# Feed-forward up stage: the first block of tokens goes through three column tiles before the second block, and three plain pairs instead of two

## The chip, the cores and the metric

One core of one Trainium2 chip. The metric is the device time of one execution in microseconds (us); the median of three runs is given, and one execution is profiled. Clock means the clock granted to TensorE: 1.00 is 2.4 GHz, the lower level is 1.2 GHz.

## The reference

Two layers of a transformer with 1024 latent tokens and, in the first layer only, 256 context tokens that are updated as well. Each layer has a mixing part and then a feed-forward part, which is where the change lies:

```python
h = modulate(rmsnorm(x, norm_ffn_g[layer]), sh2, sc2)
x = x + g2 * conv_ffn(h, ffn_w_up[layer], ffn_conv_w[layer], ffn_conv_b[layer], ffn_w_down[layer])
...
def conv_ffn(h, w_up, cw, cb, w_down):
    u = dwconv3(h @ w_up, cw, cb)
    a, b = jnp.split(u, 2, axis=-1)
    return (jax.nn.silu(a) * b) @ w_down
```

The model width is 1024, the feed-forward width 2816, all in fp32. dwconv3 is a convolution of three taps over the tokens, channel by channel.

## The kernel before

Channels lie on the 128 partitions, tokens along the free dimension: columns 0 to 255 are the context, 256 to 767 the first block of latent tokens (L0), 768 to 1279 the second (L1). Every fp32 product is made of three fp32r matmuls (mm3, lines 145 to 148): each operand is split into a high part (ScalarE, L1012 for weights, L308 for activations) and a low part (VectorE, L1013 and L309), and high x high, high x low and low x high are summed in PSUM.

The feed-forward width is cut in 22 pairs of column tiles of 128: tile j = 0 is of a, tile j = 1 of b. The document writes (i, j) for tile j of pair i. For each pair the kernel computes the product of both tiles with all tokens, runs the convolution (conv, L1026 on ScalarE, L1027 and L1029 on VectorE), the silu and the gate (L1034, L1035), and writes the result to DRAM (L1037, through the queue of SP).

norm_up (L965) comes first. It spills X to DRAM (L972) and then, block by block, makes the mean square (L262 to L267, the sum over partitions is a matmul into a tile of the pool s), the root (L270 to L275, into n_w), the scaled X (L291, in place) and its two parts hh and hl (L308, L309). The blocks are: context (layer 0 only), first block, second block. All but the last block have high priority.

up_plain (L1039) then computes NP0 = 2 pairs by plain products: pair 0 first for the context and for the first block, with both tiles, then for the second block, since the second block's hh and hl are ready last; pair 1 follows with (1,0) and then (1,1). The other 20 pairs are computed in ffn_up (L1083) by seven half-size products in place of eight (L1098 to L1100); they need the sums T1 to T4 of the blocks, which sums_b (L988) makes on VectorE and ScalarE between norm_up and up_plain in program order. T2, T3 and T4 lie in a pool pT, T1 is written over H after the plain pairs.

Weights come by up_load (L1005) into two buffers wst, and up_unit (L1016) splits a tile into whi and wlo, of which there are two each. So the split of (1,0) needs the buffer of (0,0), after that tile's last product.

PSUM has 8 banks. During up_plain they are given as uc = 1 (the context products of both tiles of a pair share it), u = 2 (tiles of two banks, one column tile each), s = 3; then s and u are closed and sx = 2, sy = 3, s = 2 are opened for ffn_up (line 1447 and below). The v tiles that the convolution writes are one per j, in a pool pV which lies where norm_up's scratch lay; a v tile is free again when the gate has read it and, for j = 0, when it has been written to DRAM.

The order of the instructions on each engine is fixed at build time by the framework's planner: it goes by its own estimate of when each instruction could start, and among those that could, by program order, with the blocks under high priority first. On the chip each engine then works through that order and waits on semaphores. In layer 0 the pairs in ffn_up also carry steps of the next layer's modulation (ada_chain, run_background; 17 steps, one a pair).

Of the kernel before, what the change touches and what calls it, by code (L numbers as in the profile page):

```python
# [8 lines left out]
F32 = mybir.dt.float32  # L9
# [5 lines left out]
P = 128  # L15
# [13 lines left out]
TB_END = [(256, 512), (768, 256), (1024, 256)]  # L29
HN = NLAT // 2  # L30
HK = KD // 2
NP0 = 2
L0, L1 = slice(NCTX, NCTX + HN), slice(NCTX + HN, T)


# [30 lines left out]
def kernel_body(ctx, tc, A, n_layers=2):  # L66
# [13 lines left out]
    def open_pool(name, side, bufs=1):  # L80
        return tc.alloc_tile_pool(name=name, bufs=bufs, side=side, reuse_waits="tile")

    def open_psum(**kinds):
        for key, bufs in kinds.items():
            PS[key] = tc.alloc_tile_pool(name="ps" + key, bufs=bufs, space=PSUM, reuse_waits="tile",
                                         side="left" if key == "s" else "right")
# [58 lines left out]
    def mm3(ps, whi, wlo, hhi, hlo, first, last):  # L145
        PE.matmul(ps, whi, hhi, start=first, stop=False)  # L146
        PE.matmul(ps, whi, hlo, start=False, stop=False)  # L147
        PE.matmul(ps, wlo, hhi, start=False, stop=last)  # L148
# [867 lines left out]
    def up_unit(i, j, c0=0):  # L1016
        hi = pW.tile([P, D], F32R, tag="whi", name="whi")
        lo = pW.tile([P, D], F32R, tag="wlo", name="wlo")
        split_w(hi[:, c0:], lo[:, c0:], raw[i, j][:, c0:])
        return hi, lo  # L1020

    def conv(l, i, j, v, u, s0, n):
        f = i + j * FT
        w = prm[l][:, PB_FCW + 3 * f:PB_FCW + 3 * f + 3]
        bi = prm[l][:, PB_FCB + f:PB_FCB + f + 1]
        S.activation(out=v[:, s0:s0 + n], in_=u, func=AF.Identity, scale=w[:, 1:2], bias=bi)  # L1026
        V.scalar_tensor_tensor(out=v[:, s0 + 1:s0 + n], in0=u[:, 0:n - 1], scalar=w[:, 0:1],  # L1027
                               in1=v[:, s0 + 1:s0 + n], op0=ALU.mult, op1=ALU.add)
        V.scalar_tensor_tensor(out=v[:, s0:s0 + n - 1], in0=u[:, 1:n], scalar=w[:, 2:3],  # L1029
                               in1=v[:, s0:s0 + n - 1], op0=ALU.mult, op1=ALU.add)  # L1030

    def gate(l, i, v, t_lo):
        a, b = v[0][:, t_lo:], v[1][:, t_lo:]
        last_silu[0] = S.activation(out=a, in_=a, func=AF.Silu)  # L1034
        V.tensor_tensor(out=a, in0=a, in1=b, op=ALU.mult)  # L1035

        (G if i == FT - 1 else SY).dma_start(out=gd[l][i, :, t_lo:], in_=a)  # L1037

    def up_plain(l, pV, tbs, wa, wb):  # L1039

        ctx_too = tbs[0][0] == 0
        w2 = [wa, wb]
        for i in range(NP0):
            pu, psc = [], None

            def product(j, t0, n):
                o = psc[:, j * NCTX:(j + 1) * NCTX] if t0 == 0 else pu[j][:, t0 - NCTX:t0 - NCTX + n]
                whi, wlo = w2[j]
                for k in range(KD):
                    mm3(o, whi[:, k * P:(k + 1) * P], wlo[:, k * P:(k + 1) * P],  # L1050
                        H[k][0][:, t0:t0 + n], H[k][1][:, t0:t0 + n], k == 0, k == KD - 1)

            v = []

            def finish(j):
                v.append(pV.tile([P, T], F32, tag=f"v{j}", name=f"v{j}"))
                with tc.high_priority():
                    if ctx_too:
                        conv(l, i, j, v[j], psc[:, j * NCTX:(j + 1) * NCTX], 0, NCTX)
                    conv(l, i, j, v[j], pu[j], NCTX, NLAT)  # L1060

            if ctx_too:
                psc = PS["uc"].tile([P, 512], F32, tag="uc", name="uc")
            for j in range(2):
                pu.append(PS["u"].tile([P, 2, 512], F32, tag="u", name="u").rearrange("p b c -> p (b c)"))
                if i == 0 and j == 1:

                    for tb in tbs:
                        product(0, *tb)
                        product(1, *tb)  # L1070
                    finish(0)
                    finish(1)
                elif i > 0:
                    for tb in tbs:
                        product(j, *tb)
                    finish(j)
            if i + 1 < NP0:
                up_load(l, i + 1)
                w2 = [up_unit(i + 1, 0), up_unit(i + 1, 1)]
            with tc.high_priority():  # L1080
                gate(l, i, v, tbs[0][0])

    def ffn_up(l, pU, Tt, tbs):  # L1083
        ctx_too = tbs[0][0] == 0
# [265 lines left out]
    for l in range(n_layers):  # L1350
# [58 lines left out]
        for p in range(3):  # L1409
# [15 lines left out]
            if p == 0:  # L1425
# [18 lines left out]
        pA.release()  # L1444

        close_psum("s", "d")
        open_psum(uc=1, u=2, s=3)
        pT = open_pool("pT", "left")
        Tt = {j: [tuple(pT.tile([P, HN], F32R, tag=f"t{j}{k}{c}", name=f"t{j}") for c in "hl") for k in range(HK)]
              for j in (2, 3, 4)}  # L1450
        pN = open_pool("pN2", "right")
        up_load(l, 0)
        wa, wb = up_unit(0, 0), up_unit(0, 1)
        norm_up(l, pN, tbs)
        pN.release()
        sums_b(l, Tt)
        pV = open_pool("pV", "right")
        up_plain(l, pV, tbs, wa, wb)
        up_load(l, NP0)
        for k in range(HK):  # L1460
            parts((H[k][0][:, L1], H[k][1][:, L1]), X[k][:, L0], None)
# [177 lines left out]
```

## Time and profile before

| | us |
|---|---|
| median of three runs | 3089.65 |
| the three runs | 3087.1, 3096.79, 3089.65 |
| the profiled execution | 3087.57 |
| its span, from the first to the last instruction | 3085.6 |
| TensorE busy | 2903.3 (94%) |
| VectorE busy | 2016.6 (65%) |
| ScalarE busy | 1271.5 (41%) |

Times in the rows are us from the start of the span. Layer 0's up stage begins at about 774, layer 1's at about 2346. A row of the timeline has start, duration, engine, line, operation, output and inputs, shape, count, and in brackets how long the engine was idle before and what released it. A matmul's duration is modelled and reaches over the start of the next one, so the pace of TensorE is read from the distance between starts.

### The profile page before, as it was taken

Reading aid. Unit: us, or ns where it says so; the run is one execution under the profiler, and the core shown is the slowest. Engines: PE = TensorE matmul, PEld = TensorE weight load, DVE = VectorE, ACT = ScalarE, POOL = GpSimd, SP = SyncE. Lnnn points to the kernel's source line nnn. Section 1 sums busy time; section 2 is a strip of 40 time slices with the busy share of each in tenths; the row PEclk is TensorE's granted clock in tenths of the full one; section 3 lists DMA queues with packets and bytes.
Section 4 is the critical chain, followed back from the end, with each engine's and each line's share of the span. In section 5 each row is a group of like instructions: output and inputs, shape, how many; then the busy total and the mean of one; then the engine's idle time right before and its main releaser. Section 6 shows DMA issues by size and latency. Waiting matters only on the chain.

```text
span 3085.6 us, 45198 instructions
## 1 busy us (share of the span) xinstructions
PE 2903.3 (94%) x17362; PEld 2343.6 (76%) x17362; DVE 2016.6 (65%) x3281; ACT 1271.5 (41%) x2350; POOL 227.8 (7%) x395
## 2 busy tenths in 40 slices
PE   6899899999899999989999799899998999998997
PEld 4676678888778888878888676677886788886886
DVE  6245664455866666768777536654548777777776
ACT  5155644354534444432112336644444444443212
POOL 0023331010000000000000003320000000000000
PEclk9999999999999999999999899999999999998998
DMA  6535556452122222243212335557532122224321
GB/s 227 159 93 164 170 175 181 126 140 86 50 88 87 88 88 88 74 158 138 93 59 82 101 100 158 166 176 200 160 90 96 69 82 82 82 82 170 117 82 55
DMA packets 258503, 361.02 MB, mean 117 GB/s; under 512 B 114288, under 2 KB 177136, under 8 KB 258288
## 3 DMA queue, kind: packets, MB, share of 16 engines
q1 hardware_dynamic: 258000, 356.95, 36.5%
q8 instruction: 137, 2.24, 0.3%
q0 software_dynamic: 288, 1.18, 0.1%
q14 instruction: 78, 0.64, 0.1%
HBM read 276.92 MB, written 81.13 MB: 116 GB/s over the span
## 4 chain that ended last, share of the span: by engine, by line
PE 74%; DVE 5%; ACT 2%; DMA 2%; issue 1%; POOL 1%; SPq 1%; DVEq 0%; ACTq 0%; POOLq 0%
PE sx L1098 5%; PE sx L1100 5%; PE sx L1099 5%; PE sy L1098 4%; PE sy L1099 4%; PE sy L1100 4%; PE uc L1099 1%; PE uc L1100 1%; PE uc L1098 1%; PE u L146 1%; PE u L147 1%; PE u L148 1%; DMA x<-xf 0%; DVE n_acc L266 0%; DVE wlo L142 0%
## 5 line engine op out<-in xcount | busy, mean ns | idle before, releaser
L141 ACT ACTIVATE whi<-wst 128x1024 fp32r<-128x1024 f32 (+1 forms) x112 | 112.7, 1023 | 465.6 <-DMA wst<-wdn 44.3
L142 DVE TENSOR_TENSOR wlo<-wst,whi 128x1024 fp32r<-128x1024 f32 (+1 forms) x112 | 132.3, 1184 | 96.6 <-ACT whi L141 94.5
L1012 ACT ACTIVATE whi<-wst 128x1024 fp32r<-128x1024 f32 x88 | 84.1, 958 | 114.8 <-PE uc L1099 70.7
L1013 DVE TENSOR_TENSOR wlo<-wst,whi 128x1024 fp32r<-128x1024 f32 x88 | 96.8, 1102 | 49.1 <-ACT whi L1012 49.1
L1012 ACT ACTIVATE s34h<-wst 128x1024 fp32r<-128x1024 f32 x40 | 42.4, 1061 | 166.5 <-PE sy L1099 163.0
L1108 DVE TENSOR_TENSOR ca<-sy,ca 128x512 f32<-128x512 f32 x80 | 55.3, 691 | 75.2 <-PE sy L1100 75.2
L1099 PE MATMUL uc<-hl,whi 128*128 128x256 f32 x320 | 90.6, 283 | 0.0
L1100 PE MATMUL uc<-hh,wlo 128*128 128x256 f32 x320 | 90.5, 283 | 0.0
L1098 PE MATMUL uc<-hh,whi 128*128 128x256 f32 x320 | 90.4, 282 | 0.0
L1037 POOL DMA_DIRECT2D gd<-v x2 | 1.4, 684 | 1168.0 <-DVE v L1035 1168.0
L1013 DVE TENSOR_TENSOR s12l<-s,s12h 128x1024 fp32r<-128x1024 f32 x40 | 49.0, 1225 | 45.5 <-ACT s12h L1012 45.5
L825 POOL TENSOR_SCALAR a_dg<-c_ident,a_sm 128x128 f32<-128x128 f32 x108 | 43.0, 398 | 444.1 <-DVE a_sm L821 311.8
L1104 ACT ACTIVATE ca<-sx 128x512 f32<-128x512 f32 x80 | 46.7, 584 | 60.0 <-PE sx L1100 60.0
L1098 PE MATMUL sx<-hh,whi 128*128 128x512 f32 x160 | 63.6, 398 | 6.2 <-DVE v L1029 6.2
L146 PE MATMUL u<-hh,whi 128*128 128x512 f32 x128 | 53.6, 428 | 15.4 <-ACT hh L308 9.5
L1098 PE MATMUL sx<-t,s12h 128*128 128x512 f32 x160 | 62.9, 393 | 2.5 <-ACT s12h L1012 2.5
L1034 ACT ACTIVATE v<-v 128x1280 f32<-128x1280 f32 (+1 forms) x44 | 51.4, 1169 | 33.0 <-DVE v L1029 32.9
L601 DVE TENSOR_TENSOR zq<-g_q,g_g 32x256 f32<-32x256 f32 x108 | 56.3, 521 | 13.1 <-ACT g_g L595 11.5
L1098 PE MATMUL sx<-t,s34h 128*128 128x512 f32 x160 | 64.4, 402 | 0.0
L265 ACT ACTIVATE n_sq<-x 128x512 f32<-128x512 f32 (+1 forms) x84 | 45.5, 552 | 44.6 <-DVE x L927 23.2
L1100 PE MATMUL sx<-hh,wlo 128*128 128x512 f32 x160 | 63.6, 397 | 0.0
L1099 PE MATMUL sx<-hl,whi 128*128 128x512 f32 x160 | 63.3, 396 | 0.0
(8035 smaller groups left out, 9892.3 us busy)
## 6 DMA issues: line engine op xcount, KB each, us to landing
wst<-wup SPq DMA_DIRECT2D x88, 512.0 KB, 3.4
ada_w<-w_ada SPq DMA_DIRECT2D x80, 512.0 KB, 4.1
wst<-win SPq DMA_DIRECT2D x48, 512.0 KB, 4.3
wst<-wdn SPq DMA_DIRECT2D x44, 512.0 KB, 3.6
f_v<-gd SPq DMA_DIRECT2D x22, 640.0 KB, 4.3
a_q<-nq SPq DMA_DIRECT2D x108, 128.0 KB, 3.7
gd<-v SPq DMA_DIRECT2D x21, 640.0 KB, 2.9
f_v<-gd SPq DMA_DIRECT2D x22, 512.0 KB, 4.2
```

The costliest lines, as they stand in the source:

```text
L141: S.activation(out=hi, in_=st, func=AF.Copy)
L142: V.tensor_tensor(out=lo, in0=st, in1=hi.bitcast(F32), op=ALU.subtract)
L146: PE.matmul(ps, whi, hhi, start=first, stop=False)
L601: V.tensor_tensor(out=zq0[r, :, g, :], in0=r3(q)[r], in1=r3(g0)[r], op=ALU.mult)
L1012: S.activation(out=hi, in_=src, func=AF.Copy)
L1013: V.tensor_tensor(out=lo, in0=src, in1=hi.bitcast(F32), op=ALU.subtract)
L1034: last_silu[0] = S.activation(out=a, in_=a, func=AF.Silu)
L1098: PE.matmul(ps, hi[:, c], bh, start=first and k == 0, stop=False, skip_group_check=True)
L1099: PE.matmul(ps, hi[:, c], bl, start=False, stop=False, skip_group_check=True)
L1100: PE.matmul(ps, lo[:, c], bh, start=False, stop=k == len(ks) - 1, skip_group_check=True)
L1104: S.activation(out=out, in_=ps, func=AF.Copy)
L1108: V.tensor_tensor(out=out, in0=ps, in1=sb, op=ALU.add)
```

## The change

It is confined to the head of the feed-forward's up stage. NP0 becomes 3. The weights of pair 1 are loaded right after the first two tiles' split, and up_third splits those of tile (1,0) in two halves into four of the eight tiles of T4's room, which T4 takes over later. up_plain becomes a generator in two parts. The first part runs the context and the first block through (0,0) and (0,1), the first block through (1,0), then the second block through (0,0) and (0,1), then the context and the second block through (1,0). T4's room is then given to T4 and sums_b runs (in program order it now stands behind the first part). The second part computes (1,1) and the third plain pair. u has three tiles instead of two, s one bank instead of three. The seven-product pairs start at pair 3.

```diff
-NP0 = 2
+NP0 = 3
...
+    def up_third(pT):
+
+        w, src = {}, raw[1, 0]
+        for k in range(HK):
+            for j, c in enumerate("hl"):
+                w[k, j] = pT.tile([P, HN], F32R, tag=f"t4{k}{c}", name="w4")
+        for i in range(2):
+            split_w(w[i, 0], w[i, 1], src[:, i * HN:(i + 1) * HN])
+        return [[w[k // HK, j][:, k % HK * P:(k % HK + 1) * P] for k in range(KD)] for j in range(2)]
+
+    def up_plain(l, pV, tbs, wa, wb, w3):
...
+        for tb in tbs[:-1]:
+            product(0, 0, *tb)
+            product(0, 1, *tb)
+        product(1, 0, *TB_LAT[0])
+        for j in range(2):
+            product(0, j, *TB_LAT[1])
+            finish(0, j)
+        if ctx_too:
+            product(1, 0, 0, NCTX)
+        product(1, 0, *TB_LAT[1])
+        yield
+        unit(1, 1)
+        up_load(l, 2)
+        end(0)
+        finish(1, 0)
+        for tb in tbs:
+            product(1, 1, *tb)
+        finish(1, 1)
+        for i in range(2, NP0):
             for j in range(2):
...
+                unit(i, j)
+            if i == 2:
+                end(1)
+            for j in range(2):
+                for tb in tbs:
+                    product(i, j, *tb)
+                finish(i, j)
...
+        end(NP0 - 1)
...
-        open_psum(uc=1, u=2, s=3)
+        open_psum(uc=1, u=3, s=1)
         pT = open_pool("pT", "left")
...
+        Tt = {j: t_rooms(j) for j in (2, 3)}
         pN = open_pool("pN2", "right")
         up_load(l, 0)
         wa, wb = up_unit(0, 0), up_unit(0, 1)
+        up_load(l, 1)
+        w3 = up_third(pT)
         norm_up(l, pN, tbs)
         pN.release()
+        pV = open_pool("pV", "right")
+        plain = up_plain(l, pV, tbs, wa, wb, w3)
+        next(plain)
+        Tt[4] = t_rooms(4)
         sums_b(l, Tt)
-        pV = open_pool("pV", "right")
-        up_plain(l, pV, tbs, wa, wb)
+        for _ in plain:
+            pass
         up_load(l, NP0)
```

product, finish, end and unit do for tile (i, j) what the loop body did before: 24 matmuls for each 512 or 256 tokens, the convolution with high priority, the gate and its write with high priority, and the split into whi and wlo.

## Rows read from the trace of the kernel before

**Rows 1.** The page: busy time by engine, and the chain of work that ended last, by engine.
```profile
PE 2903.3 (94%) x17362; PEld 2343.6 (76%) x17362; DVE 2016.6 (65%) x3281; ACT 1271.5 (41%) x2350; POOL 227.8 (7%) x395
...
PE 74%; DVE 5%; ACT 2%; DMA 2%; issue 1%; POOL 1%; SPq 1%; DVEq 0%; ACTq 0%; POOLq 0%
```

**Rows 2.** The table by stage: window and its length, busy time of each engine, granted clock, DMA share and GB/s. The first window is layer 0 from the second block's arrival to the second pair, the second the same in layer 1, the third 200 us of seven-product pairs in layer 1.
```profile
799.15:817.17 18.02, 14.42 (x48) 10.87 (x49) 16.21 (x25) 10.36 (x14) 0.00 (x0) 0.78 0.08 29
...
2368.46:2387.06 18.60, 13.21 (x48) 10.00 (x49) 18.28 (x25) 10.19 (x14) 0.00 (x0) 0.87 0.15 53
...
2500.00:2700.00 200.00, 200.00 (x884) 165.63 (x883) 156.03 (x169) 96.07 (x114) 0.00 (x0) 1.00 0.23 82
```

**Rows 3.** The timeline of TensorE at the head of the up stage, layer 0 (774 to 862) and layer 1 (2346 to 2420). 794.59 and 2360.69 are the last first-block products, 813.19 and 2381.29 the last second-block products of pair 0; 817.17 and 2387.06 begin tile (1,0), 833.49 tile (1,1) with its context product and 836.37 its first block; 847.27 and 2411.46 close the plain pairs; 2362.24 is the second block's norm sum.
```profile
794.59 0.40 PE L148 MATMUL u<-hh,wlo 128*128 128x512 f32 x1
799.15 1.22 PE L146 MATMUL u<-hh,whi 128*128 128x512 f32 x2 [4.16 <-ACT hh L308]
...
813.19 0.39 PE L148 MATMUL u<-hh,wlo 128*128 128x512 f32 x1
817.17 0.56 PE L146 MATMUL uc<-hh,whi 128*128 128x256 f32 x1 [3.59 <-DVE v L1029]
...
833.49 0.28 PE L146 MATMUL uc<-hh,whi 128*128 128x256 f32 x1
...
836.37 0.40 PE L146 MATMUL u<-hh,whi 128*128 128x512 f32 x1
...
847.27 0.28 PE L1098 MATMUL uc<-hh,whi 128*128 128x256 f32 x1
...
852.22 0.47 PE L1098 MATMUL sx<-hh,whi 128*128 128x512 f32 x1 [1.92 <-DVE v L1029]
...
2360.69 0.80 PE L148 MATMUL u<-hh,wlo 128*128 128x512 f32 x1
2362.24 1.13 PE L267 MATMUL sb__21932<-n_acc,c_ones 128*128 128x512 f32 x2 [0.76 <-DVE n_acc L266]
2368.46 1.22 PE L146 MATMUL u<-hh,whi 128*128 128x512 f32 x2 [5.09 <-ACT hh L308]
...
2381.29 0.39 PE L148 MATMUL u<-hh,wlo 128*128 128x512 f32 x1
2387.06 0.77 PE L146 MATMUL u<-hh,whi 128*128 128x512 f32 x1 [5.38 <-DVE v L1029]
...
2411.46 0.39 PE L148 MATMUL u<-hh,wlo 128*128 128x512 f32 x1
2416.16 0.47 PE L1098 MATMUL sx<-hh,whi 128*128 128x512 f32 x1 [4.32 <-DVE v L1029]
```

**Rows 4.** The timeline of VectorE (DVE) and ScalarE (ACT) in the same stretches, in order of time.
```profile
789.16 3.72 DVE L266 TENSOR_TENSOR n_acc<-n_acc,n_sq 128x512 f32<-128x512 f32 x5
796.14 0.69 DVE L273 SCALAR_TENSOR_TENSOR n_w<-sb__8284,n_w 128x512 f32<-128x512 f32 x1 [3.26 <-ACT n_w L272]
...
797.59 2.08 DVE L291 SCALAR_TENSOR_TENSOR x<-x,am,n_w 128x512 f32<-128x512 f32 x3
...
811.58 1.06 ACT L1012 ACTIVATE whi<-wst 128x1024 fp32r<-128x1024 f32 x1 [3.46 <-PE u L147]
812.55 0.54 ACT L1026 ACTIVATE v<-uc,c_prm 128x256 f32<-128x256 f32 x1
...
816.55 0.48 DVE L1029 SCALAR_TENSOR_TENSOR v<-uc,c_prm,v 128x255 f32<-128x255 f32 x1
...
2340.36 0.69 DVE L273 SCALAR_TENSOR_TENSOR n_w<-sb__21876,n_w 128x512 f32<-128x512 f32 x1 [0.59 <-ACT n_w L272]
...
2357.73 4.46 DVE L266 TENSOR_TENSOR n_acc<-n_acc,n_sq 128x512 f32<-128x512 f32 x6
...
2366.90 2.08 DVE L291 SCALAR_TENSOR_TENSOR x<-x,am,n_w 128x512 f32<-128x512 f32 x3
```

**Rows 5.** The timeline of VectorE: the last convolution step of the second tile in two neighbouring seven-product pairs, in layer 0 (two pairs without a modulation step) and in layer 1.
```profile
1320.15 1.28 DVE L1029 SCALAR_TENSOR_TENSOR v<-cb,c_prm,v 128x1023 f32<-128x1023 f32 x1
...
1345.00 1.28 DVE L1029 SCALAR_TENSOR_TENSOR v<-cb,c_prm,v 128x1023 f32<-128x1023 f32 x1
...
2631.13 1.29 DVE L1029 SCALAR_TENSOR_TENSOR v<-cb,c_prm,v 128x1023 f32<-128x1023 f32 x1
...
2650.18 1.28 DVE L1029 SCALAR_TENSOR_TENSOR v<-cb,c_prm,v 128x1023 f32<-128x1023 f32 x1
```

**Rows 6.** The timeline of SP's DMA issues: the weight loads of the up stage, the first of each row being tile (1,0)'s, in layer 0 and layer 1.
```profile
775.73 41.26 SPq L1008 DMA_DIRECT2D wst<-wup  x4
...
2348.09 36.79 SPq L1008 DMA_DIRECT2D wst<-wup  x4
```

**Rows 7.** DMA issues with KB each and median us from issue to landing, in 770 to 800 (the first row) and in 2345 to 2390.
```profile
wst<-wup SPq DMA_DIRECT2D x2, 512.0 KB, 4.9
...
wst<-wup SPq DMA_DIRECT2D x4, 512.0 KB, 3.5
```

**Rows 8.** The chain of work that ended last, in order of time (start, us, what): the first and the last of 8 neighbouring matmuls after the wait before 852.22.
```profile
853.61 0.43 PE sx L1100
...
856.60 0.43 PE sy L1098
```

More of the change, by code (lines that the diff above doesn't have):

```diff
@@ L1037, in gate @@
         (G if i == FT - 1 else SY).dma_start(out=gd[l][i, :, t_lo:], in_=a)
-    def up_plain(l, pV, tbs, wa, wb):
-        ctx_too = tbs[0][0] == 0
[L1042 to L1063, printed above, removed]
-            for j in range(2):
[L1065 to L1076, printed above, removed]
@@ new lines, in up_third, with product, finish, end @@
+    def up_third(pT):
[7 more added lines that the diff above has]
+    def up_plain(l, pV, tbs, wa, wb, w3):
+        ctx_too = tbs[0][0] == 0
+        cut = [[[t[:, k * P:(k + 1) * P] for k in range(KD)] for t in w] for w in (wa, wb)]
+        ws = {(0, 0): cut[0], (0, 1): cut[1], (1, 0): w3}
+        pu, psc, v = {}, {}, {}
+        def product(i, j, t0, n):
+            if t0 == 0:
+                if i not in psc:
+                    psc[i] = PS["uc"].tile([P, 512], F32, tag="uc", name="uc")
+                o = psc[i][:, j * NCTX:(j + 1) * NCTX]
+            else:
+                if (i, j) not in pu:
+                    pu[i, j] = PS["u"].tile([P, 2, 512], F32, tag="u", name="u").rearrange("p b c -> p (b c)")
+                o = pu[i, j][:, t0 - NCTX:t0 - NCTX + n]
+            whi, wlo = ws[i, j]
+            for k in range(KD):
+                mm3(o, whi[k], wlo[k], H[k][0][:, t0:t0 + n], H[k][1][:, t0:t0 + n], k == 0, k == KD - 1)
+        def finish(i, j):
+            v[i, j] = pV.tile([P, T], F32, tag=f"v{j}", name=f"v{j}")
+            with tc.high_priority():
+                if ctx_too:
+                    conv(l, i, j, v[i, j], psc[i][:, j * NCTX:(j + 1) * NCTX], 0, NCTX)
+                conv(l, i, j, v[i, j], pu[i, j], NCTX, NLAT)
+        def end(i):
+            with tc.high_priority():
+                gate(l, i, (v[i, 0], v[i, 1]), tbs[0][0])
+        def unit(i, j):
+            w = up_unit(i, j)
+            ws[i, j] = [[t[:, k * P:(k + 1) * P] for k in range(KD)] for t in w]
+        for tb in tbs[:-1]:
[5 more added lines that the diff above has]
+            finish(0, j)
+        if ctx_too:
+            product(1, 0, 0, NCTX)
[9 more added lines that the diff above has]
+        for i in range(2, NP0):
+            for j in range(2):
+                unit(i, j)
[5 more added lines that the diff above has]
+                finish(i, j)
@@ L1077, in up_plain @@
             if i + 1 < NP0:
                 up_load(l, i + 1)
-                w2 = [up_unit(i + 1, 0), up_unit(i + 1, 1)]
-            with tc.high_priority():
-                gate(l, i, v, tbs[0][0])
+            if i > 2:
+                end(i - 1)
+        end(NP0 - 1)
     def ffn_up(l, pU, Tt, tbs):
@@ L1446, in kernel_body, with t_rooms @@
         close_psum("s", "d")
-        open_psum(uc=1, u=2, s=3)
+        open_psum(uc=1, u=3, s=1)
         pT = open_pool("pT", "left")
-        Tt = {j: [tuple(pT.tile([P, HN], F32R, tag=f"t{j}{k}{c}", name=f"t{j}") for c in "hl") for k in range(HK)]
-              for j in (2, 3, 4)}
+        def t_rooms(j):
+            return [tuple(pT.tile([P, HN], F32R, tag=f"t{j}{k}{c}", name=f"t{j}") for c in "hl") for k in range(HK)]
+        Tt = {j: t_rooms(j) for j in (2, 3)}
         pN = open_pool("pN2", "right")
```

## The prediction

> **What bounds the kernel now.** I read the page's first parts: TensorE is busy 94% of the span and carries 74% of the chain that ended last [rows 1]. So the time is TensorE's own work plus the places where it stands still, and a change that adds matmuls can only win in such places. The table by stage finds them: in the steady part of the feed-forward TensorE is busy all the time at clock 1.00, while two stretches at the head of the up stage show 0.78 and 0.87 of the clock and less work than time, and there VectorE is the busy engine, 18.28 of 18.60 us in one of them [rows 2]. The timeline of TensorE names four waits that the change can touch [rows 3]. Two are for the second block of tokens (4.16 us in layer 0, 5.09 in layer 1, released by hh of L308), two stand at the start of the second pair (3.59 and 5.38, released by the convolution, L1029). The waits at the hand-over to the seven-product pairs (1.92 and 4.32) I expect to stay.
>
> Each wait is paid twice: after it the clock is at its lower level, 1.2 for 2.4 GHz, for some us [rows 2]. A column tile's 48 matmuls on both blocks take 847.27 - 836.37 = 10.9 us in a smooth stretch, 0.227 each. After the wait for the second block, layer 0 took 813.42 - 799.15 = 14.27 us for that much work, so 3.4 lost (some 0.5 of it is waiting for hl); layer 1 took 2381.52 - 2368.46 = 13.06, 2.2 lost. The first tile of the second pair took 833.49 - 817.17 = 16.32 in layer 0, against 847.27 - 833.49 = 13.78 for its twin: 2.5 lost. In layer 1 the second pair took 2411.69 - 2387.06 = 24.63 for 21.8: 2.8 lost [rows 3].
>
> What sets the second block's arrival is a chain through VectorE: it runs from the end of the mixing stage through the first block's modulation to the squares (789.16 + 3.72; 2357.73 + 4.46), then idles 3.26 us while TensorE sums and ScalarE makes the root, and begins the second block at 797.59 and 2366.90 [rows 4].
>
> **The change, part by part.**
>
> A third plain pair in place of a seven-product pair. A column tile costs 13.78 us with context tokens and 10.9 without, so a pair costs 27.56 and 21.8 [rows 3]. A seven-product pair costs 1345.00 - 1320.15 = 24.85 in layer 0 and 2650.18 - 2631.13 = 19.05 in layer 1 [rows 5]. Cost: 2.7 us in each layer, on the path. In layer 0 most of those pairs also carry a step of the next layer's modulation; 17 steps are spread over 20 pairs, 19 still hold them, so the price without a step is the right one.
>
> The third tile's split, earlier. Its two ScalarE and two VectorE halves (128x512 each) replace one 128x1024 split, so there is no more work, but it now stands ahead of the second block's chain on a VectorE without slack. Three VectorE operations of 128x512 take 2.08 us [rows 4], so the two cost some 1.2 once they run back to back: the second block comes 1.2 us later in each layer (bounds 0, if the 3.26 us idle takes it, and 2.5, if ScalarE's chain is held as well). The load is issued where it was before, at 775.73 and 2348.09, when the first split frees the buffer [rows 6], and lands 4.9 and 3.5 us later [rows 7]; the tile is ready near 783 and 2354, and TensorE needs it only when it has run out of the first two. On SP's queue the spills of X and this load keep their order; pair 2's second load waits there for the split of (1,1), near 813, with nothing urgent behind it. That the T4 room is taken costs nothing: T4 is first read by the first seven-product pair, now over 20 us of TensorE work later, with VectorE's sums behind the same conversions as before; if that cover were gone, one 128x512 product would wait for one split, some 1.3 us.
>
> First block through three tiles. This puts 24 x 0.227 = 5.45 us of work into the wait for the second block. Layer 0: TensorE's first-block work ended at 794.8; now it ends at 800.25, and the second block comes at 799.15 + 1.2 = 800.35. The wait is gone, and the low clock with it. Layer 1: the first-block work ended at 2360.69 + 0.4 = 2361.1 with one norm sum to come (0.9); with 5.45 more it ends at 2367.4, against 2368.46 + 1.2 = 2369.7 [rows 3]. So 2.3 us of waiting stay. The nearest row for so short a wait: after the 1.92 us before 852.22 the chain shows 8 matmuls 0.43 apart [rows 8], so I charge 8 x 0.2 = 1.6. The Trainium skill (TensorE: Matmul & The Clock Gate, HAM oscillation) has the clock fall after a spell of idleness, not at every gap; if 2.3 us is no such spell, the 1.6 goes and the time is 3068.4.
>
> Third u buffer, third column. The waits at the second pair had two causes, both held until L1029: the u buffer of the first tile (layer 1) and the single uc bank (layer 0) [rows 3]. Now 5.45 us of second-block work of tile (1,0) stand between the first pair's end and tile (1,1), the first to need an old u buffer. Layer 1: the convolution of tile (0,0) follows its product at about 2382 to 2386, and (1,1) starts at 2388: no wait. Layer 0: the uc bank was released at 816.55 + 0.48 = 817.03, by a VectorE whose order changes little [rows 4], and TensorE has second-block work until 800.35 + 0.5 + 16.35 = 817.2; the wait is between 0 and 6 us (plus 2.5 for the clock) by whether the context product is put in front of the last second-block product. I take 1, near the end where it finds other work.
>
> One s bank instead of three. Each norm sum must wait until the one before is read: layer 1's second sum ends the wait at 2362.24, the first was read at 2340.36 [rows 3, 4]. Nothing, with 20 us in hand.
>
> Sums. Layer 0: the plain pairs end at 847.27, with a seven-product pair behind them 872.12; after: 817.2 + 1 + 2.88 (context of (1,0)) + 13.78 + 27.56 = 862.4. Gain 9.7. Layer 1: before 2411.69 + 19.05 = 2430.74; after 2369.7 + 1.6 + 0.4 + 16.35 + 10.9 + 21.8 = 2420.75. Gain 10.0. Together 19.7. The profiled execution took 3087.57 us (span 3085.6), so 3067.9; the median of the runs is 2.1 higher, so 3070.0. At the bounds: split hidden (2.4), no low clock (1.6), no uc wait (1) make the gain 24.7, 3065; split at its dear end (2.6 more) and uc at its dear end (7.5 more) leave 9.6, 3080.
>
> **Rivals.**
>
> Uc in front (layer 0). The order on each engine is fixed at build time, and the context product of (1,0) comes first in the source. If it stands before the last second-block product, TensorE waits from 812 to 817 as now, at the low clock after. Gain 19.7 - 7.5 = 12.2: 3077.5.
>
> The sum behind the third tile. If the first-block product of tile (1,0) stands before the second block's norm sum on TensorE, the second block comes 5.4 us later in each layer and the wait and its clock return: 5.4 + 2.9 - 1 in layer 0 and 5.4 + 1.3 in layer 1 off the gain, 5.7 left: 3084. Against it: the norm comes earlier in the source.
>
> Slower: weights too late in a strict queue. ScalarE stood 3.46 us for one weight split with convolutions behind it [rows 4]. The Trainium skill (Perfetto Trace Analysis, Tensor Engine Instruction) calls ScalarE and VectorE strict FIFO, and the trace agrees. If the third tile's products are queued on TensorE among the first ones while its split comes only in VectorE's first idle time (after 792.9 and 2362.2), TensorE waits there with ready products behind it: the 18 us of first-block work end at 794 + 18 and 2363.4 + 18, plus 2.9 of clock each, where the forecast begins the second block at 800.85 and 2371.7. That takes 14.1 - 1 and 12.6 off the gain: 6 us slower, 3096. It decides from some 9 us of lateness on. Against it: the split has high priority, and its load lands 10 us earlier than that.
>
> No net change. The hand-over and the first seven-product pairs are replanned too, and lose there what the head gains (the waits there are 1.92 and 4.32 [rows 3]): 3088.
>
> **How the numbers follow.** Forecast 0.62 (3070, own range 3065 to 3075), uc in front 0.14, sum behind 0.09, no net change 0.08, slower 0.07. About 0.3% (9 us) is what a measurement of this kernel tells from none: the border is 3080.4. Faster: 0.62 + 0.12 of the second + 0.02 of the third = 0.76. Same: 0.02 + 0.07 + 0.07 + 0.03 = 0.19. Slower 0.05. The range: 3063 leaves little below; above it takes in the sum rival, 3085.
>
> **What would show it.** In the profile after: no wait for hh over 1 us near 800, and one of 2 to 3 us in layer 1; no wait at the start of tile (1,1) in layer 1, and at most 1 us for uc in layer 0; the second block's first hh 1.2 us later, counted from the end of the mixing stage; pairs of 24.85 and 19.05 us as before; the waits before the first sx product unchanged. It is wrong if tile (1,0)'s first-block products come after the second block's on TensorE, or if VectorE brings the second block more than 3 us later.

## The result, and the profile after

The median went from 3089.27 us (3087.1 to 3096.79, 4 runs: the three known before and a fourth of 3088.89) to 3066.78 us (3065.19 to 3073.66, 4 runs), a ratio of 0.9927 with a 95% interval of 0.9904 to 0.995. The forecast was 3070.0, and it was the case of the forecast that came, not a rival.

The profiled execution of the changed kernel was the slowest of its four (3073.66 us), and its up stage already began 6 us later than that of the kernel before (first rows of the two fences below). So the two traces are compared within the stage: from a layer's first up matmul to a mark that closes the same work in both, the last convolution step of pair 3's second tile. The timelines of TensorE and VectorE of the kernel before hold these rows (first matmul and mark, layer 0 and layer 1; in between, TensorE's later wait at the hand-over of layer 0, and the first step on the second block's n_w in layer 1):

```profile
774.03 0.39 PE L146 MATMUL uc<-hh,whi 128*128 128x256 f32 x1 [0.25 <-ACT whi L1012]
...
862.09 0.50 PE L1098 MATMUL sx<-t,s12h 128*128 128x512 f32 x1 [2.54 <-ACT s12h L1012]
...
910.52 1.28 DVE L1029 SCALAR_TENSOR_TENSOR v<-cb,c_prm,v 128x1023 f32<-128x1023 f32 x1
...
2346.04 0.50 PE L146 MATMUL u<-hh,whi 128*128 128x512 f32 x1 [0.24 <-ACT whi L1012]
...
2365.45 0.69 DVE L273 SCALAR_TENSOR_TENSOR n_w<-sb__21932,n_w 128x512 f32<-128x512 f32 x1 [3.26 <-ACT n_w L272]
...
2459.78 1.28 DVE L1029 SCALAR_TENSOR_TENSOR v<-cb,c_prm,v 128x1023 f32<-128x1023 f32 x1
```

The timeline of TensorE after, with the rows that answer to [rows 3] (tile (1,0) reads w, pair 0 and the others whi and wlo):

```profile
780.05 0.39 PE L146 MATMUL uc<-hh,whi 128*128 128x256 f32 x1 [0.24 <-ACT whi L1012]
...
807.39 0.39 PE L148 MATMUL u<-hh,w 128*128 128x512 f32 x1
807.64 0.73 PE L146 MATMUL u<-hh,whi 128*128 128x512 f32 x2
...
824.28 0.28 PE L146 MATMUL uc<-hh,w 128*128 128x256 f32 x1
...
868.99 0.28 PE L1133 MATMUL uc<-hh,whi 128*128 128x256 f32 x1
...
871.86 0.40 PE L1133 MATMUL sx<-hh,whi 128*128 128x512 f32 x1
...
880.03 0.50 PE L1133 MATMUL sx<-t,s12h 128*128 128x512 f32 x1 [2.54 <-ACT s12h L1012]
...
2343.02 0.49 PE L146 MATMUL u<-hh,whi 128*128 128x512 f32 x1 [0.25 <-ACT whi L1012]
...
2367.03 0.73 PE L146 MATMUL u<-hh,whi 128*128 128x512 f32 x2 [1.65 <-ACT hh L308]
...
2384.66 0.47 PE L146 MATMUL u<-hh,whi 128*128 128x512 f32 x1 [0.41 <-DVE v L1029]
...
2417.41 0.39 PE L1133 MATMUL sx<-hh,whi 128*128 128x512 f32 x1
...
2425.47 0.50 PE L1133 MATMUL sx<-t,s12h 128*128 128x512 f32 x1 [2.47 <-ACT s12h L1012]
```

The marks after are the last convolution step's rows on VectorE, which also shows when the second block's modulation begins (n_w of L273) and where the third tile's split stands:

```profile
787.20 1.29 DVE L1013 TENSOR_TENSOR w<-wst,w 128x512 fp32r<-128x512 f32 x2 [1.15 <-ACT w L1012]
...
804.62 0.69 DVE L273 SCALAR_TENSOR_TENSOR n_w<-sb__8292,n_w 128x512 f32<-128x512 f32 x1 [3.27 <-ACT n_w L272]
...
903.66 1.28 DVE L1029 SCALAR_TENSOR_TENSOR v<-cb,c_prm,v 128x1023 f32<-128x1023 f32 x1
...
2364.02 0.69 DVE L273 SCALAR_TENSOR_TENSOR n_w<-sb__21935,n_w 128x512 f32<-128x512 f32 x1 [3.58 <-ACT n_w L272]
...
2445.12 1.28 DVE L1029 SCALAR_TENSOR_TENSOR v<-cb,c_prm,v 128x1023 f32<-128x1023 f32 x1
```

The halves of the third tile's split on ScalarE, in layer 0 and layer 1:

```profile
786.54 1.15 ACT L1012 ACTIVATE w<-wst 128x512 fp32r<-128x512 f32 x2 [1.20 <-DMA wst<-wup]
...
2349.47 1.15 ACT L1012 ACTIVATE w<-wst 128x512 fp32r<-128x512 f32 x2 [0.52 <-DMA wst<-wup]
```

The table by stage (window, length, busy time of PE, PEld, DVE, ACT, POOL, granted clock, DMA share, GB/s) for the second block of three tiles in layer 0 and in layer 1, and for 7.5 us behind the last wait of layer 1:

```profile
807.64:824.28 16.64, 16.37 (x72) 13.08 (x71) 16.33 (x25) 10.38 (x14) 0.00 (x0) 1.00 0.13 41
...
2367.03:2384.66 17.63, 16.95 (x72) 13.25 (x73) 17.62 (x24) 10.20 (x14) 0.00 (x0) 1.00 0.17 58
2425.47:2433.00 7.53, 7.35 (x24) 5.59 (x25) 5.08 (x7) 2.72 (x3) 0.00 (x0) 0.77 0.38 139
```

What is to be seen. In layer 0 the second block begins 0.25 us behind the last first-block product: no wait, where 4.16 stood. In layer 1, 1.65 is left of 5.09. Both windows run at clock 1.00, against 0.78 and 0.87 in [rows 2]. The waits at the second pair (3.59 and 5.38) are 0 and 0.41; the context product of tile (1,0) went behind its second-block product (824.28). The waits at the hand-over (1.92 and 4.32, for v of L1029) are gone as well, which was not forecast: sx follows the product ahead of it directly. A wait for s12h (2.54) remains in layer 0 and is new in layer 1 (2.47), with a clock of 0.77 over the 7.5 us behind it there.

To the mark it is 123.61 us against 136.49 in layer 0 and 102.10 against 113.74 in layer 1: gains of 12.9 and 11.6, 24.5 together; the medians differ by 22.5. In layer 0 both stretches hold one step of the modulation, so the work is the same. What lies behind the mark is the same work too, but its time varies from trace to trace: from layer 0's mark to layer 1's first up matmul it took 1435.5 us before, 1439.4 after and 1436.8 in e8. That is why the marks are compared.

### The profile page after: what moved, and what is told of

Same layout as the page of the kernel before. It is cut to its first block, busy times and chain, and to the rows that moved or that the text cites. A ratio compares the mean times of both kernels' runs of the same rounds, so it can differ in the third digit from the quotient of the medians.

```text
span 3071.9 us, 45211 instructions
## 1 busy us (share of the span) xinstructions
PE 2901.8 (94%) x17386; PEld 2340.1 (76%) x17386; DVE 2004.4 (65%) x3265; ACT 1264.3 (41%) x2340; POOL 229.4 (7%) x395
## 4 chain that ended last, share of the span: by engine, by line
PE 72%; DVE 6%; ACT 2%; DMA 2%; SPq 2%; issue 1%; POOL 1%; DVEq 0%; ACTq 0%; POOLq 0%
PE sx L1133 5%; PE sx L1135 4%; PE sx L1134 4%; PE sy L1135 3%; PE sy L1134 3%; PE sy L1133 3%; SPq L419 1%; PE uc L1134 1%; PE uc L1135 1%; PE uc L1133 1%; PE u L147 1%; PE u L148 1%; PE u L146 1%; DVE x L927 1%; DMA x<-xf 0%
## 5 line engine op out<-in xcount | busy, mean ns | idle before, releaser
L601 DVE TENSOR_TENSOR zq<-g_q,g_g 32x256 f32<-32x256 f32 x108 | 57.1, 529 | 13.1 <-ACT g_g L595 11.5
L146 PE MATMUL u<-hh,whi 128*128 128x512 f32 x160 | 61.9, 394 | 2.8 <-ACT hh L308 1.9
L147 PE MATMUL u<-hl,whi 128*128 128x512 f32 x160 | 63.1, 396 | 1.4 <-DVE hl L309 1.4
L148 PE MATMUL u<-hh,wlo 128*128 128x512 f32 x160 | 62.7, 394 | 0.8 <-DVE wlo L1013 0.8
L1270 ACT ACTIVATE hh<-f_v 128x1280 fp32r<-128x1280 f32 (+1 forms) x36 | 41.0, 1160 | 50.5 <-DMA f_v<-gd 41.2
```

The lines of the kernel that those rows point to most:

```text
L601: V.tensor_tensor(out=zq0[r, :, g, :], in0=r3(q)[r], in1=r3(g0)[r], op=ALU.mult)
```

## The experiments

"Gain" below is always the time to the mark taken off that of the kernel before (136.49 in layer 0, 113.74 in layer 1).

**e1: the third u buffer alone.** In the kernel before:

```diff
-        open_psum(uc=1, u=2, s=3)
+        open_psum(uc=1, u=3, s=1)
```

> The kernel before with only the PSUM banks of the change: u of three tiles, s of one bank. Theory (each part of the change pays where one of the four waits stood): the wait of 5.38 us at the start of the second pair in layer 1, held by a u buffer, and its low clock go, about 8 us together; layer 0's 3.59 is held by the uc bank and may stay; the waits for the second block stay at 4.2 and 5.1 us. Total 3076 to 3082. Rival (the gain comes from the second-block waits that the third column fills): 3086 to 3089. A second question: the hand-over waits of 1.92 and 4.32 us, gone in the changed kernel; if the third u buffer took them away, they are gone here too and the total is nearer 3070 to 3074.

Measured: 3079.59 us, ratio 0.9959 (0.9942 to 0.9975), gain 8.4 and 4.4. The total is in the theory's range, but the place is only in part: some 8 us were expected in layer 1 and perhaps none in layer 0. The waits for the second block stay (4.17 and 5.09), those at the second pair are gone in both layers. With a buffer free, some 17 matmuls of tile (1,0) run ahead of its context product, which then starts at 821.47 without a wait; so the uc bank held layer 0 only while no u buffer was free. At the hand-over the timeline of TensorE has other waits:

```profile
858.19 0.80 PE L1098 MATMUL sx<-t,s12h 128*128 128x512 f32 x1 [4.48 <-ACT s12h L1012]
...
2407.94 0.47 PE L1098 MATMUL sy<-hh,whi 128*128 128x512 f32 x1 [2.73 <-DVE v L1029]
...
2415.67 0.50 PE L1098 MATMUL sx<-t,s12h 128*128 128x512 f32 x1 [3.37 <-ACT s12h L1012]
```

So the buffer frees sx from the convolution in both layers, and the next thing that is late shows: in layer 1 the room of sy, and in both the sums s12. With these waits the second question's 3070 to 3074 did not come.

**e2: the third plain pair alone.** In the kernel before:

```diff
-NP0 = 2
+NP0 = 3
```

> The kernel before with only the third plain pair (u of two tiles, order as before). Theory (the third pair is a price and nothing else): 2.7 us for each layer, all waits as before, 3094 to 3095. Rival (the third pair is what gives VectorE the time to end its sums, and so takes the hand-over waits away): those waits fall by some 6 to 9 us in all with their low clock, 3085 to 3089.

Measured: 3095.68 us, ratio 1.0014 (1.0003 to 1.0026), gain -0.3 and -3.2. Every wait stands as before (4.17, 3.60, 1.92; 5.10, 5.38, 4.32). Alone, the pair only costs, though in layer 0 less than the 2.7 expected.

**e3: the early product later in the source.** In the kernel after:

```diff
-        product(1, 0, *TB_LAT[0])
         for j in range(2):
             product(0, j, *TB_LAT[1])
             finish(0, j)
+        product(1, 0, *TB_LAT[0])
```

> The changed kernel with tile (1,0)'s first-block product put behind the second block of pair 0, so that nothing fills the wait for the second block. Theory: the wait of 4 to 6 us with the low clock returns in both layers and 5.45 us of work are paid later, some 12 to 14 us slower than the changed kernel, 3079 to 3081. Rival (the third u buffer and the hand-over carry the gain): within 4 us of the changed kernel, 3066 to 3071.

Measured: 3067.86 us, ratio 0.9922 (0.9903 to 0.9942), gain 12.8 and 13.3, with the waits of the kernel after (none in layer 0, 1.65 in layer 1). The edit did not take the filling away: nearly all of tile (1,0)'s first-block products still run ahead of the second block. Timeline of TensorE, the first of them and the second block's first:

```profile
794.65 0.40 PE L146 MATMUL u<-hh,w 128*128 128x512 f32 x1
...
801.19 0.74 PE L146 MATMUL u<-hh,whi 128*128 128x512 f32 x2
```

So the time fell where the rival had it, but the run says nothing of the rival. The planner put the ready product into the wait although its line comes later. With the third buffer but without the early split it is not ready (e5); whether it would be with the split and two buffers was not run. What the order is worth had to be found in another way (e5).

**e4: the change with two plain pairs.** In the kernel after:

```diff
-NP0 = 3
+NP0 = 2
...
-        up_load(l, NP0)
```

> The changed kernel with two plain pairs instead of three; all else as changed. Theory (the third pair is a price of 2.7 us a layer): 5.4 us faster than the changed kernel, 3061 to 3062. Rival (the third pair covers VectorE's sums, which stand later in the changed order): waits before the first seven-product pair's products return with 4 to 8 us in a layer, the low clock after them, and the total is 3066 to 3076.

Measured: 3076.72 us, ratio 0.9949 (0.9932 to 0.9966), gain 8.0 and 5.1. The rival came, with longer waits than its 4 to 8 us. The third pair's price is not seen; taking it away makes the kernel slower, by 8.9 us against e3 on the same chip and by 11.4 at the marks of the kernel after. The timeline of TensorE shows why:

```profile
853.76 0.80 PE L1133 MATMUL sx<-t,s12h 128*128 128x512 f32 x1 [8.04 <-ACT s12h L1012]
...
2410.76 0.79 PE L1133 MATMUL sx<-t,s12h 128*128 128x512 f32 x1 [10.37 <-ACT s12h L1012]
```

What TensorE saves at the head it waits for at the hand-over, where the chain that ends in s12h is not ready. In layer 0 VectorE works through the sums of the blocks and their splits until 850.5 and only then forms the first s12 (850.44 and 851.87). Without the third pair the new order gains hardly more than the buffer alone (13.1 at the marks, 12.8 in e1): the third pair is the work that covers that chain.

**e5: buffer and pair together, without the new order.** In the kernel before, both edits of e1 and e2.

> The kernel before with the two sizes changed together (three u buffers and one s bank; three plain pairs), and nothing of the new order: the first block still passes through two column tiles and the third tile's weights are split where they were. Theory (filling the wait, the third buffer and the third pair each do their part): the waits at the second pair are gone, the third pair gives VectorE its cover, so no wait or only the one for s12h at the hand-over; the waits for the second block stay at 4.2 and 5.1 us with low clock after them (3.4 and 2.2 us of clock lost). Against the kernel after it lacks 7.6 us in layer 0 and 5.6 in layer 1, but has the second block 2.5 and 1.6 us earlier in VectorE's queue, which is already in those waits: so some 9 to 13 us slower than after, 3076 to 3080. Rival (all that counts is the buffer and the pair, the filled wait comes back later behind VectorE): within 3 us of after, 3067 to 3070.

Measured: 3077.22 us, ratio 0.9954 (0.9937 to 0.997), gain 8.6 and 6.1. The timeline of TensorE:

```profile
799.14 0.86 PE L146 MATMUL u<-hh,whi 128*128 128x512 f32 x2 [4.16 <-ACT hh L308]
...
878.54 0.80 PE L1098 MATMUL sx<-t,s12h 128*128 128x512 f32 x1 [2.54 <-ACT s12h L1012]
...
2361.01 1.22 PE L146 MATMUL u<-hh,whi 128*128 128x512 f32 x2 [5.09 <-ACT hh L308]
...
2426.26 0.50 PE L1098 MATMUL sx<-t,s12h 128*128 128x512 f32 x1 [2.46 <-ACT s12h L1012]
```

The hand-over is that of the kernel after, and the waits for the second block are those of the kernel before; those at the second pair are gone, as in e1. So the hand-over belongs to the two sizes together, and the new order, with the early split in it, is worth the rest: 9.1 us by the medians (against e8, on the same chip), 10.5 by the marks. The theory's 9 to 13 held.

**e6: another room for the sums.** In the kernel after, the rooms of the seven-product stage laid out in the order v1, v0, cb, s12l, s12h, s12, zt, ca, s34l, s34h; before the edit s34l and s34h came first and the s12 rooms last:

```diff
-        for tag in ("s34l", "s34h"):
-            pU.tile([P, D], F32R, tag=tag, name=tag)
...
+        for tag in ("s34l", "s34h"):
+            pU.tile([P, D], F32R, tag=tag, name=tag)
```

> The kernel after with the order in which the rooms of the seven-product stage are laid out changed, so that the sums s12 and their split no longer lie over the plain pairs' v tiles (s34's do instead, which are needed later). Theory (the wait for s12h before the first seven-product pair's product of the sums, 2.54 and 2.47 us, comes from the room: the first sum cannot be formed until the last plain pair's gate and spill are through): the wait is gone in both layers, and the 8 matmuls at the low clock after it: 4 us each, 8 us together, 3059 beside 3067. Rival (VectorE's strict queue sets it: the sum stands behind the convolution anyway, or s34 now waits in the same way): the wait stays or turns into one for s34h of about the same length, within 2 us of after.

Measured: 3066.07 us, ratio 0.9915 (0.99 to 0.993), gain 12.7 and 12.4, the waits for s12h at 2.54 and 2.53. The theory fell: it is not the room. e10 takes the rival further.

**e7: the split's low halves on GpSimd.** In the kernel after:

```diff
-            split_w(w[i, 0], w[i, 1], src[:, i * HN:(i + 1) * HN])
+            with tc.high_priority():
+                S.activation(out=w[i, 0], in_=src[:, i * HN:(i + 1) * HN], func=AF.Copy)
+                G.tensor_tensor(out=w[i, 1], in0=src[:, i * HN:(i + 1) * HN], in1=w[i, 0].bitcast(F32), op=ALU.subtract)
```

> The kernel after with the low halves of the third tile's split on GpSimd in place of VectorE. Theory (VectorE, held for the third tile's two subtractions, is what brings the second block 2.5 and 1.6 us later): its first hh comes 1 to 2.5 us earlier in layer 0 and 1 to 1.6 in layer 1, counted from the layer's first up matmul; in layer 0 TensorE has no wait there to give back, so the time falls by what layer 1 had (1.65): 0 to 2 us, 3065 to 3067. Rival 1 (ScalarE, held for the load, is what does it, since the root of the norm stands behind it): hh within 0.5 us of after, time the same. Rival 2 (GpSimd is so slow that tile (1,0) comes late): a wait for w4 on TensorE of over 1 us and 2 us or more slower.

Measured: 3067.55 us, ratio 0.992 (0.9906 to 0.9935), gain 12.6 and 12.5. L273 comes at +24.18 and +21.37 us after the first up matmul, against +24.77 and +20.63 in e8: 0.6 won in layer 0 and 0.7 lost in layer 1, and the time is the same, as rival 1 had it. In layer 0 VectorE was spared 1.3 us of work, but it then waited 1.05 us for ScalarE, which still stood for the load, and was slower beside GpSimd (rows in the last section).

**e8: the kernel after once more.** No edit.

> The kernel after once more, on the same chip as the three others, so that they can be compared with it directly: 3065 to 3069, 0.7% faster than before. No wait for hh in layer 0 and about 1.65 us in layer 1; s12h waits of 2.5 us in both layers.

Measured: 3068.16 us, ratio 0.9919 (0.9904 to 0.9934), gain 12.8 and 12.4, waits 1.68 for hh in layer 1 and 2.54 and 2.47 for s12h.

**e9: the third tile's weights loaded ahead of the stage.** In the kernel after, with the halves as source of the split and pair 1's second tile loaded alone:

```diff
+    def third_load(l, pT):
+        for i, c in enumerate("hl"):
+            third[i] = pT.tile([P, HN], F32, tag=f"t42{c}", name="w3")
+            SY.dma_start(out=third[i], in_=A["wup"][l, 2][:, i * HN:(i + 1) * HN])
...
         up_load(l, 0)
+        third_load(l, pT)
         wa, wb = up_unit(0, 0), up_unit(0, 1)
...
```

> The kernel after with the third tile's raw weights loaded into a part of T4's room that stands empty until T4, not into the staging buffer that the first tile's split frees; so the load and the split lie in the mixing stage, ahead of the norm of the up stage. Theory (what brings the second block 2.5 and 1.6 us later is the split in the strict queues of ScalarE and VectorE, half of it work and half of it standing for the load): the first step on n_w (L273) comes at +22.1 and +19.4 us after the first up matmul, as in the kernel before; the wait for hh in layer 1 goes from 1.7 us to under 0.3, and the wait for hl of 1.0 us in the first block of layer 0 goes too: pair 3's mark 1 us earlier in layer 0 and 1.5 in layer 1, 3065 to 3066 beside 3068. Rival (the split only moves the standing to the end of the mixing stage, where VectorE adds to x with TensorE waiting for it): the first up matmul comes 1 to 3 us later in both layers and the time is the same or up to 3 us worse, 3068 to 3071.

Measured: 3061.95 us, ratio 0.9907 (0.9892 to 0.9921), gain 14.5 and 14.8. The first step on n_w on VectorE:

```profile
799.86 0.69 DVE L273 SCALAR_TENSOR_TENSOR n_w<-sb__8294,n_w 128x512 f32<-128x512 f32 x1 [3.27 <-ACT n_w L272]
...
2356.32 0.69 DVE L273 SCALAR_TENSOR_TENSOR n_w<-sb__21939,n_w 128x512 f32<-128x512 f32 x1 [3.27 <-ACT n_w L272]
```

That is +22.12 and +19.44 (less 777.74 and 2336.88), as in the kernel before to a few hundredths: the whole delay of the second block was the split and its standing for the load. The rival did not come: in the 84 us ahead of a layer's first up matmul TensorE has no wait over 0.4 us, in e9 as in e8. One expectation failed: the wait for hh in layer 1 did not go, it grew to 2.12, because TensorE's first-block work ends earlier too; its waits for wlo, hh and w (0.33, 0.40, 0.22 and 0.46 in e8) are gone. Timeline of TensorE:

```profile
2359.34 0.74 PE L146 MATMUL u<-hh,whi 128*128 128x512 f32 x2 [2.12 <-ACT hh L308]
...
2417.80 0.50 PE L1140 MATMUL sx<-t,s12h 128*128 128x512 f32 x1 [2.47 <-ACT s12h L1012]
```

The second block begins 22.46 us after the first matmul against 23.64 in e8. That is 1.2 of the 2.3 by which layer 1 beats e8; the rest is the clock behind the wait for s12h, 1.00 here and 0.79 in e8, which e9 does not explain.

**e10: one step on VectorE behind the sum.** In the kernel after; the summed step is the second half of the first sum (L1150):

```diff
-                V.tensor_tensor(out=s[:, n_:], in0=s[:, :n_], in1=a[:, :n_], op=ALU.subtract)
+                summed[0] = V.tensor_tensor(out=s[:, n_:], in0=s[:, :n_], in1=a[:, :n_], op=ALU.subtract)
...
-                add_out(ca[:, :HN], y, ca[:, :HN])
+                with tc.issue_after(summed[0].ins) if i == NP0 else ExitStack():
+                    add_out(ca[:, :HN], y, ca[:, :HN])
```

> The kernel after with one order put on VectorE at the first seven-product pair: the step that adds the second product out of sy (L1143), which in layer 0 stands between the two halves of the first sum and waits 1.7 us there for TensorE, comes behind the second half. Layer 1 has that order already. Theory (in layer 0 the wait for s12h is TensorE waiting for its own product, by way of that step): the wait of 2.54 us goes to under 0.5, and the 8 matmuls 0.43 us apart behind it go: 3.5 to 4 us in layer 0, none in layer 1, 3064 beside 3068. Rival 1 (ScalarE sets it: the conversion of s12 stands behind copies out of sx and a convolution): the wait stays above 1.5 us. Rival 2 (the sum is late anyway, behind the convolution and the gate): the wait falls by at most 0.7, the length of that step.

Measured: 3065.16 us, ratio 0.9915 (0.9901 to 0.993), gain 14.9 and 12.4. The timeline of VectorE at the hand-over of layer 0, first in e8, then in e10:

```profile
870.33 0.68 DVE L1149 TENSOR_TENSOR s<-wst 128x512 f32<-128x512 f32 x1
872.68 0.69 DVE L1143 TENSOR_TENSOR ca<-sy,ca 128x512 f32<-128x512 f32 x1 [1.68 <-PE sy L1135]
873.29 0.68 DVE L1150 TENSOR_TENSOR s<-s,wst 128x512 f32<-128x512 f32 x1
```

```profile
869.55 0.68 DVE L1149 TENSOR_TENSOR s<-wst 128x512 f32<-128x512 f32 x1
870.26 0.69 DVE L1150 TENSOR_TENSOR s<-s,wst 128x512 f32<-128x512 f32 x1
871.91 0.69 DVE L1143 TENSOR_TENSOR ca<-sy,ca 128x512 f32<-128x512 f32 x1 [0.95 <-PE sy L1135]
```

In e8 the sum stands behind a step that waits for TensorE, and TensorE then waits for the sum. In e10 the wait for s12h is 0.30 and the clock behind it 1.00, as the theory said; but of 3.5 to 4 us only 2.1 came, because the next wait is close behind (timeline of TensorE in e10):

```profile
872.10 0.50 PE L1133 MATMUL sx<-t,s12h 128*128 128x512 f32 x1 [0.30 <-ACT s12h L1012]
...
874.59 0.64 PE L210 MATMUL sb__9262<-ada_w,cT 128*32 128x256 f32 x8 [1.29 <-DMA ada_w<-w_ada]
```

**e11: the first sum ahead of the last convolution.** In the kernel after, the seven-product stage's rooms opened earlier, with the last plain pair's v tiles in them, and the sum put before its two convolutions and its gate:

```diff
...
-                finish(i, j)
+                if i < NP0 - 1:
+                    finish(i, j)
...
+        pool[0] = yield
+        finish(NP0 - 1, 0)
+        finish(NP0 - 1, 1)
         end(NP0 - 1)
...
+        s_first = sums12(NP0, pU)
+        try:
+            plain.send(pU)
...
```

> The kernel after with the rooms of the seven-product stage opened ahead of the last plain pair's convolution and gate, whose v tiles lie there too, and the first sum s12 formed ahead of them on VectorE. Theory (the sum stands behind the convolution and the gate only because of the order of the queue; its loads are there): no wait for s12h in either layer (2.54 and 2.46 before), no low clock behind it: 4 us in each layer, 3060 beside 3068. Rival (VectorE has no slack there: the convolution, now later, holds the u buffers over which sx and sy lie, or the uc bank, and TensorE waits for L1029 at the hand-over as in the kernel before): a wait for sx, sy or uc of 1 us or more in place of the one for s12h, 3066 to 3072.

Measured: 3082.59 us, ratio 0.997 (0.9958 to 0.9981), gain 9.0 and 5.8. The rival came by its kind of wait, but the time is far above its 3066 to 3072. Timeline of TensorE:

```profile
875.47 0.55 PE L1158 MATMUL uc<-hh,whi 128*128 128x256 f32 x1 [6.33 <-DVE v L1029]
...
2427.40 0.77 PE L1158 MATMUL sx<-hh,whi 128*128 128x512 f32 x1 [7.80 <-DVE v L1029]
```

No wait for s12h is left, but the edit moved more than the sum: the convolution of tile (2,0) now also stands behind the copies of T1 (L981, L982), for which ScalarE stands 8.19 us (for plain products of TensorE's) and VectorE behind it 7.59 in layer 0 (2.76 and 2.70 in layer 1), and uc and sx wait for it. So it shows what a late convolution costs here, not what the sum alone would give.

**e12: e9 and e10 together.**

> The kernel after with the edits of e9 and e10 together: the third tile's raw weights in T4's empty room ahead of the stage, and the step on sy behind the first sum. If the two are independent, as the theory has it (one acts at the head of the stage, the other at its hand-over): 4.1 us from e9 (1.7 in layer 0, 2.3 in layer 1) and 2.1 from e10 in layer 0, so 6.2 against after: 3061 to 3062 by the profiles, 3060 by the medians, a ratio to the kernel before of 0.990. Rival (what e9 gives comes back at the hand-over, where VectorE has no slack, as e11 showed): 3065 or more, and a wait for v, s12h or whi at the hand-over longer than in e10.

Measured: 3062.36 us, ratio 0.9905 (0.9886 to 0.9924), gain 16.4 and 13.2, 29.6 together against 25.2 in e8 and 29.3 in e9; of the 6.2 expected against the kernel after 4.4 came. L273 comes at +22.13 and +19.40; the waits are 0.30 for s12h and 1.40 for ada_w in layer 0, 2.11 for hh and 2.46 for s12h in layer 1, there with the clock at 0.79 again, so that layer 1 is behind e9 by 1.6. By the medians it stands with e9 (3061.95), and both some 5 us ahead of the kernel after; the intervals of their ratios overlap with its.

## Why the prediction was right, step by step

**The filled wait** held in its place and nearly in its size. The forecast had the second block of layer 0 begin 26.3 us after the first up matmul (800.35 less 774.03) with no wait and no low clock; it began at 27.59 (807.64 less 780.05), and so it was but for the delay below. In layer 1 it was 23.7 against 24.01 measured, with 1.65 of wait where 2.3 was forecast. e5 shows the same without the order: 4.16 and 5.09 come back, and 9 to 10.5 us with them. The "sum behind the third tile" and the "weights too late" rivals are out: the second block's start did not move by 5 us or more.

**The third tile's split** was the mis-sized term. 1.2 us was taken, between bounds of 0 and 2.5; L273 came 2.46 later in layer 0 (24.57 less 22.11) and 1.59 in layer 1 (21.00 less 19.41). The work was near (1.29 us on VectorE; the row that the 1.2 was read from, 2.08 for three, gives 1.4 for two), but the two halves were taken to run as soon as they came up, and they came up before their load: ScalarE stood 1.20 us for it in layer 0 and 0.52 in layer 1, VectorE behind it 1.15 in layer 0. 1.29 and 1.15 make nearly all of the 2.46. The bound spoke of ScalarE's chain, the taken value left it out. e9 takes load and split out of the stage and the delay is 0.0; e7 takes only VectorE's share and wins nothing over both layers. The Trainium skill (Perfetto Trace Analysis, Tensor Engine Instruction) has ScalarE and VectorE take their work strictly in order, and these waits agree with it. The price was set by the load's landing, which the trace alone gives.

**The clock after the short wait** in layer 1 was charged at 1.6 us and cost nothing: the window behind it runs at 1.00. This is the case the forecast left open with the Trainium skill (TensorE: Matmul & The Clock Gate, HAM oscillation), where a short gap is no such spell. The length of the wait alone does not decide it, though: 1.92 us in the kernel before [rows 8] and 2.5 us for s12h had low clock behind them (last section).

**Uc** was allowed 1 us and waited 0: the context product went behind the last second-block product, so the rival "uc in front" did not come. The wait at layer 1's second pair went to 0.41, as the times of the convolution had it. But the uc bank was not a cause by itself: e1 takes layer 0's 3.59 away and leaves that bank as it was.

**The third pair's price**, 2.7 a layer, was near for the pair alone in layer 1 (e2: 3.2). In layer 0 it was 0.3: some 1.5 came back, since the clock behind the first wait recovered sooner in that trace (0.90 where the kernel before had 0.78), and the rest is open. But the step that VectorE's sums stand "behind the same conversions as before", over 20 us of TensorE's work ahead of their use, was silent on the pair being that cover. In the new order with two pairs TensorE waits 8.04 and 10.37 for s12h (e4). In the sum this does no harm, as the change has three pairs.

**The hand-over** was forecast as it was, and gave 5.0 us: 3.7 in layer 0 and 1.3 in layer 1. This is the one step that failed outright. To the end of the plain pairs and one seven-product pair's time the forecast was 9.7 and 10.0, and the stage gave 9.2 and 10.3 (before, 847.27 - 774.03 + 24.85 = 98.09 and 2411.69 - 2346.04 + 19.05 = 84.70; after, 868.99 - 780.05 = 88.94 and 2417.41 - 2343.02 = 74.39), 19.5 against 19.7; the rest of the 24.5 came behind that. The waits of 1.92 and 4.32 were for a u buffer under sx, and the third buffer takes that away as it does at the second pair: e1 shows it with only the two counts of banks changed. The forecast had applied the third buffer to the second pair only. What then ends last is s12h, in layer 0 through a step of VectorE's that waits for TensorE itself (e10); in layer 1 e10's order already stood, and what sets its 2.47 was not tried alone.

That 3070.0 came within 3.3 us of the median is therefore partly luck: the delay was too small by 1.7, allowances of 2.6 (the clock and uc) were not needed, and a gain of 5 was missed, which together would make 6 us more than forecast; 4.8 of them show at the marks and 2.8 in the medians.

## What to carry to other kernels

A wait at the head of a stage can be filled with the next tile's first part if three things come together: a buffer for its result, its weights ready before the wait, and enough work later to cover the engine that is now behind. Here the buffer alone gave 12.8 of the 24.5 us at the marks, by other waits (e1), the extra work alone cost 3.5 (e2), and the new order without that work added 0.3 to the buffer (e4); the order without the buffer was not run. When a buffer is added, look for every place where something waits for that ring, also where the next stage takes over its room. And put a load far enough ahead of the conversion that reads it, for on a queue in order a conversion that stands for its load delays all that is behind it, however urgent.

## What the runs showed of the hardware

The same wait of TensorE left the clock high in some executions and low in others. Behind the wait of 2.46 to 2.53 us for s12h in layer 1 the granted clock over 8 us was 0.79 in six kernels (the kernel after, e5, e6, e8, e10, e12) and 1.00 in three (e3, e7, e9). The table by stage, in e8 and then in e9:

```profile
2417.55:2425.55 8.00, 8.00 (x28) 6.40 (x29) 5.52 (x7) 3.32 (x4) 0.00 (x0) 0.79 0.38 131
```

```profile
2417.80:2425.80 8.00, 7.82 (x33) 6.18 (x34) 5.61 (x7) 3.20 (x4) 0.00 (x0) 1.00 0.39 131
```

e9 and e12, alike up to that wait, are 1.6 us apart at layer 1's mark. Behind the wait of 2.54 us for s12h in layer 0 the clock was 0.79 to 0.81 in every kernel that has it (nine). Behind waits of 1.65 to 2.12 us for hh in layer 1 it was 1.00. What decides it is open. So the clock's part in the gain of a single trace is not to be counted on.

In e7 VectorE was slower beside GpSimd. Three steps of L309 take 2.07 us elsewhere in that trace; beside GpSimd's two subtractions they took 3.12. Timeline of GpSimd, then of VectorE, in e7 (beside GpSimd, and right behind):

```profile
780.80 2.99 POOL L1048 TENSOR_TENSOR w<-wst,w 128x512 fp32r<-128x512 f32 x2 [66.89 <-ACT w L1047]
```

```profile
781.89 3.12 DVE L309 SCALAR_TENSOR_TENSOR hl<-x,mod,hh 128x512 fp32r<-128x512 f32 x3 [1.05 <-ACT hh L308]
...
786.91 2.07 DVE L309 SCALAR_TENSOR_TENSOR hl<-x,mod,hh 128x512 fp32r<-128x512 f32 x3
```

The Trainium skill (SBUF — State Buffer, Who interferes with whom) has these two engines share a pair of ports that one holds against the other; the 1.05 us longer agrees with that.
